# Batched matrix product on Trainium2: one store moves to GpSimd's DMA queue, and SyncE's list of transfers is regrouped into longer blocks

## Chip, cores and metric

The kernel runs on one core of a Trainium2 chip. The metric is the device time of one execution in microseconds (us). Profiles show one execution each; traces give every instruction, every DMA's issue, and the landings of its parts.

## What is computed

For each of 16 batches the kernel multiplies a 512 x 512 float32 matrix by the transpose of another. The core of the reference is

```python
batch, m, k, n = 16, 512, 512, 512
a, b: float32 (16, 512, 512)
out = np.matmul(a, b.transpose(0, 2, 1)).astype(np.float32)
```

The inputs are 33.55 MB and the output is 16.78 MB; each byte crosses between HBM and on-chip memory once. The kernel casts to bfloat16 before it multiplies and sums in float32.

## The kernel before

**Tiles.** The kernel works on 8 pairs of batches. Below, load 2u brings the two a matrices of pair u and load 2u+1 its two b matrices, so there are loads 0 to 15, each of 2 MiB. Store n writes output matrix n, 1 MiB, so there are stores 0 to 15; pair u makes outputs 2u and 2u+1. Loads 0 and 1 are issued in two halves of 1 MiB each (L98, L101), the others whole (L105). All stores are issued at L110. The landing buffer `ld` has NL = 7 slots, the output buffer `ob` has NO = 7 slots, and both are used in turn.

**Engines.** VectorE (DVE) casts each load to bfloat16 in four pieces (L155 to L163), and copies the transposed b tiles out of PSUM (L175). TensorE (PE) transposes the tiles against an identity (L235) and multiplies (L254). ScalarE (ACT) copies the transposed a tiles (L194) and the products into `ob` (L212). PE, DVE and ACT each run a loop of 8 rounds, one per pair, and meet through semaphores.

**Queues.** SyncE (SP) issues all 34 DMAs, one after another, in the order that the string ORDER spells out by hand: an L is the next load, an S the next store. Where a load reuses a slot, SP first waits on `s_cd` until DVE has begun on the load after the one that held the slot. Before store n it waits on `s_out` until n+1 outputs stand in `ob`. A waiting SP issues nothing that stands behind it in the list.

**GpSimd as messenger.** GpSimd (POOL) walks the same list. For each load it waits for the landing (`s_ld`) and passes it on to DVE as `s_go`. For each of the stores 0 to 8 it waits for the landing (`s_st`) and passes it on to ACT as `s_of`, a count of free `ob` slots. ACT starts with 7 of them and takes two ahead of each pair's output copies. GpSimd issues no DMA in the kernel before.

The lines that set the order:

```python
ORDER = "LLLLLLLSSLLLLSLSSLSLSLLSSSSSSSSS"
...
if n_ld >= NL:
    nc.sync.wait_ge(s_cd, n_ld - NL + 2)
...
nc.sync.wait_ge(s_out, n_st + 1)
nc.sync.dma_start(out[n_st]..., ob[:, slot]).then_inc(s_st[slot], 16)
```

Of the kernel before, what the change touches and what calls it, by code (L numbers as in the profile page):

```python
# [10 lines left out]
def kernel(  # L11
# [6 lines left out]
    nc = tc.nc  # L18
    P = 128
    batch, M, K = a.shape  # L20
    _, N, _ = b.shape
    J = M // P
# [6 lines left out]
    NL = 7  # L29
    NO = 7  # L30


    ORDER = "LLLLLLLSSLLLLSLSSLSLSLLSSSSSSSSS"

    def sbuf(name, shape, dtype):
        return ctx.enter_context(nc.sbuf_tensor(name, shape, dtype))

    def sem(name):
        return tc.alloc_semaphore(name)

    with tc.tile_critical(no_gpsimd_drain=True):  # L41
# [8 lines left out]
        ob = sbuf("ob", [P, NO, J, N], f32)  # L50
# [3 lines left out]
        s_set = sem("s_set")  # L54
        s_ld = [sem(f"s_ld{i}") for i in range(NL)]
        s_second = [sem(f"s_second{i}") for i in range(2)]
        s_st = [sem(f"s_st{i}") for i in range(NO)]

        s_go = sem("s_go")
        s_of = sem("s_of")  # L60
# [12 lines left out]
        s_out = sem("s_out")  # L73
# [5 lines left out]
            out=ident[:], in_=ident[:], compare_op=mybir.AluOpType.not_equal, fill=1.0,  # L79
# [4 lines left out]

        n_ld = n_st = 0
        for what in ORDER:
            if what == "L":
                u, slot = n_ld // 2, n_ld % NL  # L90
# [21 lines left out]
                ).then_inc(s_st[slot], 16)  # L112
                n_st += 1
        for n in range(batch - NO, batch - 1):
            nc.sync.wait_ge(s_st[n % NO], 16 * (n // NO + 1))


        n_ld = n_st = 0
        for what in ORDER:
            if what == "L":  # L120
                got = nc.gpsimd.wait_ge(s_ld[n_ld % NL], 16 * (n_ld // NL + 1))
                if n_ld < 2:
                    got.then_inc(s_go, 1)
                    nc.gpsimd.wait_ge(s_second[n_ld], 16).then_inc(s_go, 1)
                else:
                    got.then_inc(s_go, 2)
                n_ld += 1
            else:
                if n_st < batch - NO:
                    nc.gpsimd.wait_ge(  # L130
                        s_st[n_st % NO], 16 * (n_st // NO + 1)
                    ).then_inc(s_of, 1)
                n_st += 1

# [11 lines left out]
        with nc.Fori(0, pairs, engines=[dve]) as u:  # L146
            for x, (h, w, s_c, s_w) in enumerate(
# [4 lines left out]
                if x == 0:  # L152
# [3 lines left out]
                    out=h[:, :J, :], in_=src[:, :J, :HK]  # L156
# [4 lines left out]
                    out=h[:, J:, :], in_=src[:, J:, :HK]  # L161
                ).then_inc(s_c, 1)
                nc.vector.tensor_copy(  # L163
                    out=w[:, J:, :], in_=src[:, J:, HK:]
                ).then_inc(s_w, 1)
            for ko in range(KO):
# [5 lines left out]
                if ko == 1:  # L172
# [3 lines left out]
                    out=tb[:, ko, :],  # L176
# [9 lines left out]
        with nc.Fori(0, pairs, engines=[act]) as u:  # L186
            for ko in range(KO):
# [5 lines left out]
                for e in range(2):  # L193
                    c = nc.scalar.copy(  # L194
                        out=ta[:, ko, e * J * P:(e + 1) * J * P].rearrange(
                            "k (j p h) -> k j p h", j=J, h=2
                        ),
# [6 lines left out]
            for e in range(2):  # L204
                dst = ob[:, bass.ds((u * 2 + e) % NO, 1)].rearrange("m o j n -> m (o j) n")
                for j in range(J):
                    if j < J - 1:
                        nc.scalar.wait_ge(s_mm, j + 1)
                    else:
# [3 lines left out]
                        out=dst[:, j, :].rearrange("m (p j) -> m p j", j=2 * J),  # L213
# [51 lines left out]


    with tc.tile_critical(no_gpsimd_drain=True):
        nc.sync.wait_ge(s_st[(batch - 1) % NO], 16 * ((batch - 1) // NO + 1))


# [28 lines left out]
```

## Time and profile before

| what | value |
|---|---|
| median of 4 runs | 127.22 us (127.1 to 127.5) |
| profiled execution, its own time | 127.38 us |
| its span, first to last instruction | 125.6 us |
| time around the span in that execution | 1.78 us |
| DMA queue of SyncE | 50.33 MB, 96.1% of 16 DMA engines' span |
| mean rate over the span | 401 GB/s |
| PE / DVE / ACT / POOL busy | 74% / 56% / 54% / 1% |
| last store: issued, landed | 116.0 us, 124.2 us |

Busy shares are averages over the span. The time is read against the profiled execution's own 127.38 us: the span and the 1.78 us around it.

### The profile page before, as it was taken

The numbers are of one execution on the slowest core, as the hardware profiler recorded it, in microseconds if no ns is written. First come the engines' busy times: TensorE is split into PE (matmuls) and PEld (weight loads), VectorE is DVE, ScalarE is ACT, GpSimd is POOL, SyncE is SP. The second block draws the span as 40 slices with busy tenths as digits, with TensorE's granted clock in tenths as the row PEclk, the third lists the DMA queues.
The fourth block names the chain that finished last, engine by engine and source line by source line (L and its number), as shares of the span: only waits on it lengthen the run. The fifth ranks groups of instructions, "written<-read, shape, count | busy, mean of one in ns | idle before, by whom it ended". The sixth has DMA issues, their size and how long they took to land. (4 is left out here: it accounts for less than half of the span.)

```text
span 125.6 us, 2407 instructions
## 1 busy us (share of the span) xinstructions
PE 93.2 (74%) x768; PEld 58.6 (47%) x768; DVE 70.3 (56%) x112; ACT 68.3 (54%) x130; POOL 0.7 (1%) x6
## 2 busy tenths in 40 slices
PE   0005299998999899799989998995079998997000
PEld 0005296457447644664475467443078447642000
DVE  0056676937992891988768568370486858500000
ACT  4004133669558946965595679568106559566000
POOL 2000000000000000000000000000000000000000
PEclk9999999999999999999999999999757999999965
DMA  3999999999999999999999999999999999999970
GB/s 89 399 425 433 444 438 418 433 428 433 438 295 397 446 391 438 428 433 423 423 428 444 397 454 397 384 451 418 438 428 438 412 418 433 423 425 425 428 321 18
DMA packets 4896, 50.33 MB, mean 401 GB/s; under 512 B 544, under 2 KB 544, under 8 KB 544
## 3 DMA queue, kind: packets, MB, share of 16 engines
q1 hardware_dynamic: 4896, 50.33, 96.1%
HBM read 33.55 MB, written 16.78 MB: 401 GB/s over the span
## 5 line engine op out<-in xcount | busy, mean ns | idle before, releaser
L254 PE MATMUL ps<-tb,ta 128*128 128x512 bf16 x256 | 58.1, 381 | 0.4
L212 ACT COPY ob<-ps 128x512 f32 x64 | 34.7, 588 | 26.9 <-PE ps L254 26.9
L194 ACT COPY ta<-tp 128x512 bf16<-128x512 bf16 x64 | 32.9, 604 | 19.8 <-PE tp L235 19.8
L254 PEld LDWEIGHTS ps<-tb,ta 128*128 128x128 bf16 x256 | 24.4, 98 | 30.7 <-issue 4.1
L235 PE MATMUL tp<-ident,ha 128*128 128x128 bf16 x256 | 20.2, 236 | 12.8 <-PEq L136 12.5
L235 PE MATMUL tp<-ident,hb 128*128 128x128 bf16 x256 | 19.8, 239 | 8.8 <-PEq L136 8.7
L235 PEld LDWEIGHTS tp<-ident,ha 128*128 128x128 bf16 x256 | 17.5, 106 | 16.0 <-issue 14.4
L175 DVE COPY tb<-tp 128x1024 bf16<-128x1024 bf16 x32 | 21.3, 685 | 5.5 <-DVEq L136 5.4
L235 PEld LDWEIGHTS tp<-ident,hb 128*128 128x128 bf16 x256 | 17.6, 108 | 9.5 <-issue 9.5
L155 DVE CAST hb<-ld 128x1024 bf16 x8 | 5.5, 693 | 12.7 <-DVEq L136 12.5
L155 DVE CAST ha<-ld 128x1024 bf16 x8 | 5.5, 689 | 9.5 <-DVEq L136 9.4
L170 DVE COPY ha<-wa 128x2048 bf16<-128x2048 bf16 x8 | 5.6, 694 | 8.4 <-DVEq L136 8.1
L160 DVE CAST hb<-ld 128x1024 bf16 x8 | 5.5, 686 | 1.1 <-DVEq L136 1.1
L160 DVE CAST ha<-ld 128x1024 bf16 x8 | 5.5, 686 | 1.0 <-DVEq L136 1.0
L174 DVE COPY hb<-wb 128x2048 bf16<-128x2048 bf16 x8 | 5.5, 685 | 0.5 <-DVEq L136 0.5
L158 DVE CAST wa<-ld 128x1024 bf16 x8 | 5.5, 686 | 0.0
L163 DVE CAST wa<-ld 128x1024 bf16 x8 | 5.5, 685 | 0.0
L158 DVE CAST wb<-ld 128x1024 bf16 x8 | 5.5, 685 | 0.0
L163 DVE CAST wb<-ld 128x1024 bf16 x8 | 5.5, 685 | 0.0
L185 ACT ACT_TABLE_LOAD x1 | 1.3, 1283 | 1.1 <-SPq L41 1.1
L78 POOL TENSOR_SCALAR_AFFINE_SELECT ident<-ident 128x128 bf16<-128x128 bf16 x1 | 0.3, 294 | 0.2 <-POOL ident L76 0.2
L76 POOL MEMSET ident<- 128x128 bf16 x1 | 0.2, 205 | 0.5 <-SPq L41 0.5
(5 smaller groups left out, 0.6 us busy)
## 6 DMA issues: line engine op xcount, KB each, us to landing
out_dram<-ob SPq DMA_DIRECT2D x16, 1024.0 KB, 27.6
ld<-in_a_dram SPq DMA_DIRECT2D x7, 2048.0 KB, 30.5
ld<-in_b_dram SPq DMA_DIRECT2D x7, 2048.0 KB, 29.5
ld<-in_a_dram SPq DMA_DIRECT2D x2, 1024.0 KB, 6.4
ld<-in_b_dram SPq DMA_DIRECT2D x2, 1024.0 KB, 10.4
```

The costliest lines, as they stand in the source:

```text
L155: nc.vector.tensor_copy(out=h[:, :J, :], in_=src[:, :J, :HK]).then_inc(s_cd, 1)
L158: nc.vector.tensor_copy(out=w[:, :J, :], in_=src[:, :J, HK:])
L160: nc.vector.tensor_copy(out=h[:, J:, :], in_=src[:, J:, :HK]).then_inc(s_c, 1)
L163: nc.vector.tensor_copy(out=w[:, J:, :], in_=src[:, J:, HK:]).then_inc(s_w, 1)
L170: nc.vector.tensor_copy(out=ha[:], in_=wa[:]).then_inc(s_ca, 1)
L174: nc.vector.tensor_copy(out=hb[:], in_=wb[:]).then_inc(s_cb, 1)
L175: nc.vector.tensor_copy(out=tb[:, ko, :], in_=tp[:, 2 + ko % 2].rearrange("k j p -> k (j p)"),).then_inc(s_eb, 1)
L185: nc.scalar.copy(out=one[:], in_=nc.const_aps.tensor(1.0, (P, 1), f32))
L194: c = nc.scalar.copy(out=ta[:, ko, e * J * P:(e + 1) * J * P].rearrange("k (j p h) -> k j p h", j=J, h=2), in_=tp[:, ko % 2, :, e * HP:(e ...
L212: c = nc.scalar.copy(out=dst[:, j, :].rearrange("m (p j) -> m p j", j=2 * J), in_=ps[:, j, :].rearrange("m (j p) -> m p j", j=2 * J),)
L235: t = nc.tensor.transpose(tp[:, 2 * x + g, j, :], h[:, j, g * P:(g + 1) * P], ident[:])
L254: t = nc.tensor.matmul(ps[:, j, :], ta[:, ko, (e * J + j) * P:(e * J + j + 1) * P], tb[:, ko, :].rearrange("k (j p) -> k j p", j=2 * J)[:, ...
```

## The change

Store 0 is taken out of SP's list. GpSimd issues it: after it has passed on load 3 it waits until output 0 is in `ob` (`s_out` at 1), starts the DMA on its own queue with a semaphore of its own (`s_first`), goes on to loads 4 to 6, and after load 6 waits for the landing of store 0 and passes that on to ACT.

SP's list becomes 9 loads, stores 1 to 3, 5 loads, stores 4 to 6, 2 loads, stores 7 to 15. Since slot 0 of `ob` has one store fewer on its semaphore, a small function gives the count that marks a landing. Tiles, casts, transposes, products and copies are as before.

```diff
-    ORDER = "LLLLLLLSSLLLLSLSSLSLSLLSSSSSSSSS"
+    ORDER = "LLLLLLLLLSSSLLLLLSSSLLSSSSSSSSS"
...
+        s_first = sem("s_first")
...
+        def landed(n):
+            return 16 * (n // NO + (n % NO > 0))
...
-        n_ld = n_st = 0
+        n_ld, n_st = 0, 1
...
                     got.then_inc(s_go, 2)
                 n_ld += 1
+                if n_ld == 4:
+                    nc.gpsimd.wait_ge(s_out, 1)
+                    nc.gpsimd.dma_start(
+                        out[0].rearrange("(p j) n -> p j n", j=J), ob[:, 0]
+                    ).then_inc(s_first, 16)
+                elif n_ld == NL:
+                    nc.gpsimd.wait_ge(s_first, 16).then_inc(s_of, 1)
...
-                        s_st[n_st % NO], 16 * (n_st // NO + 1)
+                        s_st[n_st % NO], landed(n_st)
```

More of the change, by code (lines that the diff above doesn't have):

```diff
@@ L114 @@
         for n in range(batch - NO, batch - 1):
-            nc.sync.wait_ge(s_st[n % NO], 16 * (n // NO + 1))
-        n_ld = n_st = 0
+            nc.sync.wait_ge(s_st[n % NO], landed(n))
+        n_ld, n_st = 0, 1
         for what in ORDER:
@@ L267 @@
     with tc.tile_critical(no_gpsimd_drain=True):
-        nc.sync.wait_ge(s_st[(batch - 1) % NO], 16 * ((batch - 1) // NO + 1))
+        nc.sync.wait_ge(s_st[(batch - 1) % NO], landed(batch - 1))
 _INS = ['a', 'b']
```

## The prediction

> **What bounds the kernel now.** I read the page's engine shares and DMA line first, then the time in windows, then SyncE's waits and issues.
>
> ```profile
> PE 93.2 (74%) x768; PEld 58.6 (47%) x768; DVE 70.3 (56%) x112; ACT 68.3 (54%) x130; POOL 0.7 (1%) x6
> ...
> DMA  3999999999999999999999999999999999999970
> GB/s 89 399 425 433 444 438 418 433 428 433 438 295 397 446 391 438 428 433 423 423 428 444 397 454 397 384 451 418 438 428 438 412 418 433 423 425 425 428 321 18
> ...
> q1 hardware_dynamic: 4896, 50.33, 96.1%
> ```
>
> No compute engine is over 74% busy, while the 16 DMA engines are at 9 tenths or more from slice 2 to the last but one. So the kernel is one stream of 48 MiB, and its time is the stream's length. The stream works first in, first out: loads 2 to 5 land at 18.63, 23.52, 28.43 and 33.33 us, 4.90 us per 2 MiB, and in the last nine stores 2.46 us go by per MiB (means over 16 parts). A transfer takes its bytes and nothing besides. Only dips in the rate lengthen the stream. These are windows over them (columns: window, us, busy of PE, PEld, DVE, ACT, POOL, clock, DMA share, GB/s):
>
> ```profile
> 34.30:37.50 3.20, 3.20 (x17) 1.45 (x15) 3.20 (x6) 1.92 (x4) 0.00 (x0) 1.00 1.03 328
> 44.30:46.30 2.00, 1.94 (x10) 0.81 (x9) 2.00 (x5) 1.07 (x2) 0.00 (x0) 1.00 0.98 352
> 66.50:68.00 1.50, 1.50 (x16) 0.84 (x13) 1.19 (x2) 1.01 (x3) 0.00 (x0) 1.00 1.10 459
> 76.40:79.40 3.00, 2.81 (x37) 2.12 (x36) 2.50 (x5) 2.62 (x6) 0.00 (x0) 1.00 0.96 363
> 8.00:34.30 26.30, 20.61 (x171) 14.58 (x172) 18.10 (x30) 13.08 (x26) 0.00 (x0) 1.00 1.01 431
> 84.00:86.00 2.00, 2.00 (x17) 1.10 (x15) 0.79 (x2) 1.40 (x4) 0.00 (x0) 1.00 1.02 434
> 90.00:94.00 4.00, 2.28 (x22) 2.31 (x23) 3.56 (x7) 0.00 (x0) 0.00 (x0) 0.50 1.01 434
> ```
>
> The undisturbed rate is 431. In the dips the share stays near 1: engines hold load packets that take longer, they don't stand idle. The lost time is 3.20 x (1 - 328/431) = 0.76 us at 34 us, 2.00 x (1 - 352/431) = 0.37 at 44 us, 3.00 x (1 - 363/431) = 0.47 at 76 us, 1.6 in sum. The first lies within load 6, before any store moves. The other two lie 1 to 3 us behind a block of two stores (0 and 1; 3 and 4). Behind single stores (2, 5 and 6: windows at 66, 84 and 90) nothing is lost.
>
> ```profile
> SPq L110 <- ACT ob L212: 89.0, 16, 20.4
> SPq L105 <- DVE ha L155: 3.4, 1, 3.4
> ...
> 26.21 2.52 SPq L110 DMA_DIRECT2D out_dram<-ob  x2
> ...
> 63.53 52.84 SPq L110 DMA_DIRECT2D out_dram<-ob  x9
> ```
>
> SP waits 89 us for outputs, and it costs nothing: what it issues then waits in the stream anyway (27.6 us from issue to landing in the median store). The last two stores are issued at 113.86 and 116.04 us and land 7.9 and 8.2 us later. An empty queue needs 5.35 us (first half load, 0.94 to 6.29). So output 15 could come 8.2 - 5.35 = 2.8 us later without moving the end.
>
> **What the Trainium skill says.** The page "DMA: Bandwidth & Descriptors", section "Issuing engines are not separate DMA queues", says that transfers from SP, ACT and GpSimd run on the same 16 engines and interleave. The trace before has one queue alone, so the sharing isn't shown; that the engines are full is (96.1%). Its section "Queues, rings and completion order" says that an engine takes turns between queues, packet by packet; no run here shows it yet. The page "SBUF — State Buffer", section "SBUF: two separate sides", says that a GpSimd DMA's descriptors wait while VectorE holds the shared port in a two-port copy. In the trace DVE's casts end at 26.36 us and its next work starts at 28.68, so store 0's issue near 26.2 meets a free port. The page "TensorE: Matmul & The Clock Gate", Part 1, says that the clock halves after an idle window of about 3.4 us. The trace agrees: after PE idles 5.08 us up to 91.72, the 90 to 94 window has clock 0.50.
>
> **The change, part by part.** The sum is made against the profiled execution: 125.6 + 1.78 around it = 127.38 us, 0.16 over the median. I apply the difference to the median, 127.22.
>
> *Bytes and issues.* 48 MiB stay 48 MiB. SP loses one issue of 0.34 us and one wait, POOL gains them; both stand beside the full stream. Cost 0.
>
> *Cover of SP's new order.* Loads 7 and 8 leave earlier: their slots are free at about 12.3 and 21.9 us (DVE's casts of loads 1 and 2), against 28.78 and 29.25. Then SP waits for stores 1, 2, 3 (28.4, 37.7, 39.9 us) and all of loads 9 to 13 stand behind that. By 39.9 the stream has moved about 15 of the 22 MiB issued, so 7 x 2.45 = 17 us of work cover the wait. The next block, stores 4 to 6, is issued by about 61 us with some 12 MiB ahead of it. Load 15 waits for the cast of load 9, near 65 us; the stream then has 10 MiB left. No gap, cost 0. Were this cover gone, each us of SP's wait would be a us of time.
>
> *Store 0 on GpSimd.* POOL waits from load 3 (23.5 us) until output 0 at 26.2; load 4 lands at 28.43 and its casts start at 32.87, so 4 us hide it. Its 1 MiB goes in turns with load packets from about 27 to 35 us; load 5 slips from 33.3 to about 35.8. Pair 2's transposes of b start at 39.82, the four casts take 2.8, so this is hidden too. Bounds for its own cost to the stream: upper 0.4 us, an estimate from the first-byte times in the same DMA page's "Latency and other measured facts" (about 1 us against 0.6), if engines stood idle for it, which loads behind them speak against; lower -0.76, if its packets filled the first dip, although they should be through before most of it. I take 0.
>
> *Later landings for ACT.* Load 9 moves from MiB 22 to 24 of the stream (59.2 to 64 us), store 4 from 29 to 33 (76.5 to about 86.5). ACT's copies of pair 5 began at 80.32; they now wait for slot 4, until about 86.7. Eight copies with PE between them took 6.2 us there; with the first products ready some 5.2 suffice, so pair 5 ends near 92 instead of 86.53. Load 13 is 2 MiB earlier (34 to 32, near 84 us), so pair 6 starts at once and, at a pair per 11.51 us (transposes start at 38.93 and 50.44), ends near 103.5, against 104.51. Pair 7 hangs on load 15, MiB 39 in both orders, so it ends near 116 again. If PE idles into a half-clock window on the way (3.4 us more), about 118.4, within the 2.8 us. Cost 0.
>
> *Switches of direction.* 11 changes between loads and stores become 5 in SP's list. By themselves they cost nothing visible: DMA share and rate hold through 82 to 90 us, where four of them lie. What cost time were dips behind blocks: pairs 0.37 + 0.47 = 0.84, singles 0. Now there are two blocks of three ahead of loads. Lower bound: a block of three costs what one of two does, 0.42 each, 0.84 in all, difference 0. Upper: the third store adds as much again as the second, 0.84 each, 1.68, difference +0.84. I take the middle, +0.42, as no row decides. The dip of 0.76 in load 6 has no store ahead of it, and I let it stand.
>
> Sum: 0 + 0 + 0 + 0 + 0.42, so 127.22 + 0.42 = 127.6 us.
>
> **Rivals.** *Nothing moves.* Dips saturate with two stores, or are HBM's own and come with load bytes, which are the same: 127.2 us. For it: the dip in load 6 needs no store. Against: all others follow pairs.
>
> *Faster, by fewer and shorter dips* (the other side). The dip before the first store block, 0.76 us, is tied to how the first stores meet the loads, or store 0's packets fill it: 127.22 - 0.76 = 126.5. Or the cost is per return to loads: 0.84 over five returns is 0.17, two remain, -0.5, 126.7. For it: the dip ends just as the first stores begin. It decides from the point that dips in the after add up to less than 1.4 us. Against: singles cost nothing, so a cost per switch does not fit.
>
> *Compute catches up with the stream.* The wait for store 4 and two half-clock windows (2 x 3.4 us) take pair 7's end from 116 to 122.8; less the 2.8 of slack, +4 us at most; half of that is 129.2. It decides once output 15 is later than 118.8 us. Against: load 13's earlier landing gives most of it back.
>
> That the change doesn't do what it says is hardly possible: the order of issues is written out.
>
> **How the numbers follow.** Longer dips (127.3 to 128.4, likeliest 127.6): 0.42. Nothing: 0.20. Faster: 0.33. Compute: 0.05. About 0.2%, 0.25 us, is what a measurement of this kernel can tell from no change. Faster 0.33, same 0.20, slower 0.42 + 0.05 = 0.47. The range takes in the faster case to 126.3 (126.5 less the 0.2 by which runs vary) and the longer dips with their upper bound, 0.84, and the 0.4 of GpSimd's first byte: 127.22 + 1.24 = 128.5. The likeliest case's own range is 127.3 to 128.4.
>
> **What would show it.** Right: DMA share full throughout; the rate under 380 for some 3 us after stores 1 to 3 (around 60 us) and after 4 to 6 (around 92); last issue near 116. Wrong: a queue beside q1 whose packets take much longer than 0.31 us per 8 KB; no dips after the blocks; 34 to 38 us at 430 GB/s; a gap in the DMA line near 40 or 60 us; the last store issued after 118.8.

## The result, and the profile after

The changed kernel takes 127.05 us (median of 42 runs, 126.24 to 127.57) against 127.47 us for the kernel before on the same chips (63 runs, 126.53 to 128.44; the 127.22 on record was the median of the first four). The ratio is 0.9969, with a 95% interval of 0.9955 to 0.9984: faster by 0.31%, some 0.4 us; small, but the interval leaves out 1. The forecast was slower, 127.6.

The profiled execution took 126.81 us, its span is 125.0. These are the shares and the DMA line of its page:

```profile
PE 92.4 (74%) x768; PEld 57.6 (46%) x768; DVE 70.1 (56%) x112; ACT 68.2 (55%) x130; POOL 1.4 (1%) x7
...
DMA  3999999999999999999999999999999999999970
GB/s 84 396 425 448 430 430 430 435 430 364 417 425 435 451 425 401 425 425 427 409 440 440 419 430 425 425 414 422 438 414 430 406 419 433 425 427 425 422 309 31
...
q1 hardware_dynamic: 4752, 49.29, 94.0%
q0 software_dynamic: 144, 1.05, 2.0%
```

The kernel is the same full stream as before. GpSimd's queue is q0: 2.0% of the span is 2.5 us per engine for 1 MiB, what a store on SP's queue takes too. The slice of 295 GB/s (slice 12 before) is gone; a shallower one, 364, stands in slice 10, from 28 us on, around the start of store 0, whose own packets run beside the loads from 29.79 to 37.72 us. The windows over the dips (columns as before: window, us, PE, PEld, DVE, ACT, POOL busy, clock, DMA share, GB/s):

```profile
8.00:28.00 20.00, 14.92 (x117) 10.78 (x118) 12.93 (x20) 8.64 (x17) 0.67 (x1) 1.00 1.01 432
28.00:33.50 5.50, 4.95 (x57) 3.36 (x55) 4.89 (x8) 4.21 (x9) 0.00 (x0) 1.00 1.00 387
34.30:37.50 3.20, 3.20 (x16) 1.44 (x15) 2.21 (x4) 2.05 (x4) 0.00 (x0) 1.00 1.00 428
57.80:60.80 3.00, 3.00 (x16) 1.35 (x15) 0.02 (x1) 2.15 (x4) 0.00 (x0) 1.00 0.98 377
90.60:92.60 2.00, 2.00 (x34) 1.82 (x32) 0.47 (x1) 1.87 (x4) 0.00 (x0) 1.00 1.03 401
```

Against 431 GB/s, as in the prediction, the losses are 0.56 us (28 to 33.5), 0.02 (34 to 37.5), 0.38 behind stores 1 to 3 and 0.14 behind stores 4 to 6: 1.1 us, where the kernel before lost 1.6. The dip in load 6 has not stayed, and the dips behind the blocks of three did not grow.

SyncE's issues after (start, us, queue, line, count; merged rows include the waits between):

```profile
12.26 0.33 SPq L110 DMA_DIRECT2D ld<-in_b_dram  x1
21.70 0.33 SPq L110 DMA_DIRECT2D ld<-in_a_dram  x1
27.83 11.84 SPq L115 DMA_DIRECT2D out_dram<-ob  x3
...
64.85 0.34 SPq L110 DMA_DIRECT2D ld<-in_b_dram  x1
```

Loads 7, 8 and 15 leave at 12.26, 21.70 and 64.85 us, and no slice of the DMA line falls below 9 in between: SP's long waits are covered.

### The profile page after: what moved, and what is told of

The parts are those of the page before. It is cut to its first block, busy times and chain, and to the rows that moved or that the text cites. A ratio compares the mean times of both kernels' runs of the same rounds, so it can differ in the third digit from the quotient of the medians.

```text
span 125.0 us, 2407 instructions
## 1 busy us (share of the span) xinstructions
PE 92.4 (74%) x768; PEld 57.6 (46%) x768; DVE 70.1 (56%) x112; ACT 68.2 (55%) x130; POOL 1.4 (1%) x7
## 5 line engine op out<-in xcount | busy, mean ns | idle before, releaser
L247 PE MATMUL tp<-ident,hb 128*128 128x128 bf16 x256 | 19.1, 234 | 7.6 <-PEq L148 7.5
L247 PEld LDWEIGHTS tp<-ident,hb 128*128 128x128 bf16 x256 | 17.1, 106 | 8.3 <-issue 8.3
L135 POOL DMA_DIRECT2D out_dram<-ob x1 | 0.7, 668 | 24.2 <-ACT ob L224 24.2
## 6 DMA issues: line engine op xcount, KB each, us to landing
out_dram<-ob SPq DMA_DIRECT2D x15, 1024.0 KB, 21.9
```

The lines of the kernel that those rows point to most:

```text
L247: t = nc.tensor.transpose(tp[:, 2 * x + g, j, :], h[:, j, g * P:(g + 1) * P], ident[:])
```

## The experiments

Three questions were put: which half of the change gives the gain, whether dips follow the order or chance, and what the first one hangs on. "Dip" below is the time lost in a window, its length times (1 - rate/431), from one profile of each kernel. Ratios are against the kernel before on the same chip, with 95% intervals.

The windows are picked by eye and leave things out. From 37.5 to 41 us, where stores 0 and 1 run in the kernel before, its two profiles show 389 and 410 GB/s, which is another 0.34 and 0.17 us that the table does not count. So a measure that picks nothing stands beside them: the landing of store 15, the last. It has 16 parts. Their mean says how long the stream took, and the execution ends some time after the last part. The column gives the mean, and how far behind it the last part came.

| kernel | what differs from before | first dip | all dips | store 15 lands: mean + last part behind it | ratio | interval |
|---|---|---|---|---|---|---|
| before, two profiles | | 0.76, 0.82 | 1.60, 1.26 | 122.28 + 1.94, 122.08 + 1.60 | 1 | |
| changed kernel, two profiles | both halves | 0.56, 0.45 | 1.08, 0.89 | 121.72 + 1.93, 121.64 + 1.94 | 0.9969 | 0.9955 to 0.9984 |
| blocks_only | SP's list alone | 0.26 | 0.85 | 121.81 + 1.77 | 0.9966 | 0.9948 to 0.9985 |
| pool_only | store 0 on GpSimd alone | 0.56 | 1.13 | 121.73 + 2.26 | 0.9952 | 0.9919 to 0.9984 |
| act_loads | second queue without GpSimd | 0.33 + 0.28 | 1.16 | 121.76 + 1.50 | 0.9953 | 0.9929 to 0.9978 |
| alternate | seven single stores, 7 returns | 0.73 | 1.38 | 122.04 + 1.93 | 0.9987 | 0.9972 to 1.0002 |
| eight_first | first store behind 8 loads | 1.01 | 2.15 | 122.49 + 1.35 | 0.9981 | 0.9960 to 1.0001 |
| nine_first | first store behind 9 loads | 0.38 | 1.32 | 121.93 + 1.93 | 0.9979 | 0.9961 to 0.9998 |
| prewrite | 64 KB stored early | 0.65 | 1.38 | 122.34 + 2.63 | 1.0003 | 0.9977 to 1.0029 |
| pool_early | stores 0 to 6 on GpSimd | 0.45 | 0.50 | 121.52 + 1.17 | 0.9895 | 0.9874 to 0.9916 |
| pool_spread | the same, stores 4 to 6 later | 0.38 | 0.53 | 121.16 + 1.89 | 0.9892 | 0.9868 to 0.9916 |

(The 0.28 of act_loads lies from 37.5 to 41 us, the stretch that is not counted for the others.) In the changed kernel's two profiles the mean comes 0.36 to 0.64 us earlier than in the two of the kernel before. The trace's packets say where: those of loads 2 to 15 took 70.1 and 70.0 us per engine in the kernel before and 69.6 in both profiles of the changed one, those of the stores 39.7 in all four.

### Each half alone

```diff
# blocks_only, in the kernel before
-    ORDER = "LLLLLLLSSLLLLSLSSLSLSLLSSSSSSSSS"
+    ORDER = "LLLLLLLLLSSSSLLLLLSSSLLSSSSSSSSS"
# pool_only, in the changed kernel
-    ORDER = "LLLLLLLLLSSSLLLLLSSSLLSSSSSSSSS"
+    ORDER = "LLLLLLLSLLLLSLSSLSLSLLSSSSSSSSS"
```

> The regrouped list alone: store 0 goes back into SyncE's list, at the head of its first block, so 9 loads, 4 stores, 5 loads, 3 stores, 2 loads, 9 stores, no DMA on GpSimd. Against 127.47 us for the kernel before. If the gain comes from fewer returns from stores to loads (2 in place of 5): 127.0, and a dip before the first store remains. If it comes from store 0 going beside the loads: no gain, 127.4 to 127.5. If longer blocks cost more, as the prediction had it (a block of four 1.0 to 1.3 us of dip behind it): 127.9 or more.

> Store 0 alone on GpSimd's queue, the rest of SyncE's list as in the kernel before less its first store: 7 loads, store 1, 4 loads, store 2, load, stores 3 and 4, and so on. If the gain comes from store 0 beside the loads: 127.0, and load 6 shows no dip. If it comes from fewer returns to loads: no gain, 127.4 to 127.5, since the 5 returns stay.

Measured: 127.04 and 126.65 us against 127.38. Each half alone gives about the whole gain, and the two do not add up: the intervals of all three kernels overlap. Their windows between 28 and 47 us, first blocks_only, then pool_only:

```profile
34.30:37.50 3.20, 3.20 (x16) 1.46 (x15) 3.17 (x6) 1.92 (x5) 0.00 (x0) 1.00 1.00 425
44.30:46.80 2.50, 2.48 (x12) 1.19 (x13) 2.50 (x5) 1.33 (x3) 0.00 (x0) 1.00 1.05 387
```

```profile
28.00:33.50 5.50, 4.95 (x55) 3.28 (x53) 4.97 (x9) 4.21 (x10) 0.00 (x0) 1.00 0.99 387
34.30:37.50 3.20, 3.20 (x17) 1.45 (x15) 2.18 (x4) 2.13 (x4) 0.00 (x0) 1.00 1.01 430
```

Both lack the dip at 34 us. In blocks_only it has moved with the first store to load 8, and is smaller (0.26 us); in pool_only it lies around the start of store 0 beside the loads (0.56). What is left later, 0.59 and 0.57 us, differs little, though blocks_only returns twice to loads and pool_only five times. Blocks of four and three stores (0.38 and 0.21 behind them) cost no more than pairs did: the prediction's "longer blocks" is refuted here.

### Order or chance, returns or pairs

before_again and after_again are the two kernels unchanged, for a second profile.

> The kernel before, unchanged, for a second profile of it. If dips sit where the order of transfers puts them: again a dip of 0.7 to 0.9 us in load 6, near 34 to 37 us, ahead of the first store, and some 0.3 us each behind stores 1 and 4. If dips come by chance: in other loads, of other sizes.

> The changed kernel, unchanged, for a second profile of it. If dips sit where the order puts them: again about 0.5 us of longer load packets between 28 and 33 us, where store 0 goes beside the loads, none at 34 to 37, about 0.3 behind store 3 near 58 us and 0.2 behind store 6 near 91. If by chance: elsewhere.

The line of the first dip in before_again:

```profile
34.30:37.50 3.20, 3.20 (x17) 1.42 (x16) 2.87 (x5) 2.08 (x4) 0.00 (x0) 1.00 1.00 320
```

The dips came again in the same places: before 0.82, 0.37 and 0.07 us, after 0.45, 0.30 and 0.14. The large ones hold their size; the one at 76 us does not (0.47, then 0.07). The profiled execution of before_again took 126.84 us, about as long as those of the changed kernel (126.81 and 126.75): its mean landing is later than theirs, but its last part came only 1.60 us behind the mean. A single execution's time therefore does not tell the kernels apart; the medians and the mean landings do.

The next kernel, stream_before, has no computation at all; DVE only fills the output buffer once, which shifts the stream by 15 us, and it takes 142.29 us.

```diff
-                    nc.sync.wait_ge(s_cd, n_ld - NL + 2)
+                    nc.sync.wait_ge(s_ld[slot], 16 * (n_ld // NL))
...
-                nc.sync.wait_ge(s_out, n_st + 1)
```

> Leaves out all the computation: no casts, transposes, products or copies, the stores send a constant, and loads wait only for the landing of the load that held their slot. SyncE's list is that of the kernel before. If dips come from the order of loads and stores in the stream: dips of the same size in load 6 and behind the store pairs, 1.5 us in sum. If they come from the engines' work beside the stream, or from what waits on it: no dips but at the start.

Its windows (window, us, DVE, POOL busy, clock, DMA share, GB/s):

```profile
23.00:49.00 26.00, 0.00 (x0) 0.00 (x0) 1.00 1.02 433
49.00:53.00 4.00, 0.00 (x0) 0.00 (x0) 1.00 0.95 303
59.00:62.00 3.00, 0.00 (x0) 0.00 (x0) 1.00 1.01 366
64.00:80.00 16.00, 0.00 (x0) 0.00 (x0) 1.00 1.01 433
```

15 us later than in the kernel before come a first dip (49 to 53 for 34 to 38) and one behind the pair (59 to 62 for 44 to 47), with PE, DVE and ACT idle. They are 1.19 and 0.45 us, not smaller than the 0.76 and 0.37 of before. So the dips belong to the order of loads and stores in the stream, not to the engines' work beside it.

alternate spreads the first seven stores singly:

```diff
-    ORDER = "LLLLLLLSSLLLLSLSSLSLSLLSSSSSSSSS"
+    ORDER = "LLLLLLLSLSLSLSLSLSLLSLLSSSSSSSSS"
```

> The kernel before with its first seven stores each alone between loads, 7 returns to loads and no pair of stores ahead of a load, nothing on GpSimd. If each return costs some 0.15 us: slower than before by about 0.3 us, 127.8. If only blocks of two and more cost, as the prediction had it: the 0.84 us behind the pairs go, 126.7. If dips come by chance whatever the order: 127.4 to 127.5 with dips anywhere in the loads.

127.13 us against 127.38, not told from no change. Its dips are 0.73 ahead of the first store, then 0.26, 0.25 and 0.14 behind stores 0, 1 and 2, and none behind stores 3 to 6 (427 GB/s from 70 to 78 us). The window behind store 0:

```profile
41.00:44.00 3.00, 2.81 (x34) 1.81 (x30) 2.50 (x5) 2.32 (x5) 0.00 (x0) 1.00 1.02 393
```

Single stores do cost, if they are early. Neither the number of returns alone nor the length of a block alone sets the price. Being late does not make a return free either: the pair of stores 3 and 4, near 76 us, costs 0.30 to 0.47 us in six of the seven profiles that have it there, and 0.07 in before_again (skewed and skew_clean, which come below, apart). No rule that holds in all profiles was found.

### What the first dip hangs on

eight_first and nine_first move only the place of the first pair of stores:

```diff
-    ORDER = "LLLLLLLSSLLLLSLSSLSLSLLSSSSSSSSS"
+    ORDER = "LLLLLLLLSSLLLSLSSLSLSLLSSSSSSSSS"    # eight_first
+    ORDER = "LLLLLLLLLSSLLSLSSLSLSLLSSSSSSSSS"    # nine_first
```

> The kernel before with one load moved: 8 loads ahead of the first two stores and 3 behind them, all else the same, 5 returns, nothing on GpSimd. If the gain hangs on where the first store meets the loads (a dip that the first store of the list causes, smaller when that store comes later): faster by 0.3 to 0.4 us, about 127.1. If it hangs on the number of returns or on block lengths: no gain, 127.4 to 127.5.

> The kernel before with two loads moved: 9 loads ahead of the first two stores and 2 behind them, all else the same, 5 returns, nothing on GpSimd. The regrouped list alone had its first dip in load 8 and only half as large (0.39 us against 0.85). If the place of the first store decides: a dip of about 0.4 us in load 8, and 127.1 us. If the block length behind it decides (four stores there, two here): a dip of 0.8 in load 8, as with 8 loads first in load 7 (0.81), and 127.4.

The dips of 0.39, 0.85 and 0.81 us in the second expectation are counted by packets: the time that load packets in the dip took over their usual 0.611 us, per engine. These are the windows of the first dips, eight_first's and then nine_first's:

```profile
39.00:43.00 4.00, 3.45 (x43) 2.34 (x41) 3.50 (x7) 3.25 (x7) 0.00 (x0) 1.00 0.95 322
44.30:47.00 2.70, 2.70 (x14) 1.27 (x13) 2.70 (x6) 1.87 (x4) 0.00 (x0) 1.00 1.01 370
```

127.23 us against 127.56, not told from no change, and 127.06 against 127.38, just told from it. The first dip follows the store each time, to 39 to 43 us and to 44 to 47. It is 1.01 us behind eight loads, not smaller than behind seven, and 0.38 behind nine. So nine loads ahead of the store halve the dip with no long block behind it. But the dips behind the stores are then larger (0.94 in sum, against 0.59 in blocks_only); the gain, 0.21%, is not told from that of blocks_only, 0.34%.

eight_first has more dips than the kernel before and yet is no slower. Its landings resolve this for its one profile: the mean is the latest of the kernels without added transfers, 122.49 us, as its dips would have it, but the last part came only 1.35 us behind it, where before had 1.94 and 1.60. In that execution the parts were already closer together at load 2, ahead of every store: 0.31 us against 0.63 and 0.50.

prewrite stores 64 KB of zeros to a corner of output 15, behind load 3; the whole of output 15 is stored over it later.

```diff
+                if n_ld == 4:
+                    nc.sync.wait_ge(s_fill, 1)
+                    nc.sync.dma_start(
+                        out[batch - 1].rearrange("(p j) n -> p j n", j=J)[:, 0, :P], pre[:]
+                    ).then_inc(s_pre, 16)
```

> The kernel before with a small extra store: 64 KB of zeros to a corner of output 15 go out right behind load 3, near 23 us, and output 15 is stored over it at the end. The 64 KB themselves add about 0.2 us to the stream. If the dip in load 6 is a cost of the very first write to HBM, paid once: it moves to 20 to 24 us, and load 6 at 34 to 37 us runs at the full 430 GB/s. If it belongs to the first full store behind a row of loads: it stays at 34 to 37 us and the time is 0.2 above that of before, 127.6.

127.66 against 127.56 us. 426 GB/s from 20 to 25 us, and 343 from 34.3 to 37.5: the dip stays. It isn't the price of the first write to HBM as such, at least not of a small one.

act_loads gives the first loads to ScalarE's queue, so that SP's first stores need not stand behind them:

```diff
+                queue = nc.scalar if n_ld < NL else nc.sync
...
-                    nc.sync.dma_start(ld[:, slot], src).then_inc(s_ld[slot], 16)
+                    queue.dma_start(ld[:, slot], src).then_inc(s_ld[slot], 16)
```

> The kernel before with loads 0 to 6 issued by ScalarE ahead of its other work, all else by SyncE in the order of before, nothing on GpSimd. Stores 0 and 1 then go beside loads 4 to 6 on a second queue that is not GpSimd's. If a second queue is what makes the first store cheap: longer load packets of 0.4 to 0.5 us around 27 to 33 us, none at 34 to 37, and 126.7 to 127.1. If it takes GpSimd's queue: a dip of 0.8 us and no gain, 127.4.

126.7 us against 127.5, and no dip at 34 to 37.5 us:

```profile
34.30:37.50 3.20, 3.20 (x16) 1.47 (x15) 2.01 (x4) 2.05 (x4) 0.00 (x0) 1.00 1.01 430
```

So a second queue gives the gain without GpSimd issuing anything.

skewed and skew_clean put three small loads on 8 of the 128 partitions behind load 4, to set some engines back:

```diff
+                if n_ld == 5:
+                    for i in range(4, NO):
+                        nc.sync.dma_start(
+                            ob[:8, i], a[0, :8 * J].rearrange("(p j) k -> p j k", j=J)
+                        ).then_inc(s_skew, 16)
```

They land in slots 4 to 6 of `ob`, which ACT may use only afterwards. skew_clean reads rows 520 apart instead (about 1 MiB).

> The kernel before with three small extra loads behind load 4: 8 KB on each of 8 partitions, to output slots not yet in use, so that some of the 16 engines fall behind the others by up to 0.93 us; added work, nothing left out. If dips arise because the engines go in step (spread of a landing under 1 us) when they change from loads to stores and back: the first dip, 0.8 us in load 6, shrinks to under 0.3, and the time is at most 127.5 in spite of 0.5 us of added packets. If the order alone makes the dip: it stays at 0.8 us and the time goes to 128 or more.

> As skewed, but the small extra loads (8 KB on each of 8 partitions, three times) read rows of the input that lie about 1 MiB apart, so that they should not hinder each other; added work, nothing left out. If the first dip is paid once, when engines first come apart: the small loads take it, little or nothing of it is left in load 6 before the first store at 38 us, and the sum of longer load packets is 1.2 us or less. If the first full store causes it: 0.8 us in load 6 as in the kernel before, on top of what the small loads cost.

130.18 and 130.46 us, ratios 1.023 (1.0194 to 1.0266) and 1.0209 (1.0178 to 1.024). As a saving, the idea failed: the small loads stretch the packets around them, whichever of the two sets of rows they read. Windows of skew_clean:

```profile
26.50:31.50 5.00, 4.51 (x62) 3.44 (x59) 3.79 (x7) 4.40 (x9) 0.00 (x0) 1.00 1.01 203
34.30:37.50 3.20, 3.20 (x17) 1.43 (x16) 0.47 (x1) 1.91 (x5) 0.00 (x0) 1.00 1.01 430
45.50:48.00 2.50, 2.50 (x13) 1.15 (x12) 0.73 (x2) 1.22 (x4) 0.00 (x0) 1.00 1.07 406
```

The price is 2.65 us at 26.5 to 31.5, but afterwards load 6 runs at 430 with the first stores right behind it, and the dip behind the pair is down to 0.15 us. Both kernels show this. That fits a price paid once, by whatever disturbs the stream first. It does not show that the price is for the engines coming apart, which was the idea. How far a load's last part lands behind the mean of its 16 parts tells how far apart they are. Across the first dip this grew in the kernel before (0.64 to 0.99 us, in the second profile 0.50 to 0.66), but it shrank in eight_first (0.31 to 0.24), nine_first (0.31 to 0.21) and blocks_only (0.32 to 0.24), and jumped there only one step later, at the first load behind the stores, to 0.80, 0.69 and 0.92. What the first dip pays for stays open.

### A faster version

pool_early issues stores 0 to 6 from GpSimd as they become ready, SP has 16 loads and then 9 stores; pool_spread holds stores 4 to 6 back until load 11 has landed. GpSimd's list of what it waits for and issues (L: pass on a load, i: issue a store, w: pass on its landing):

```diff
+        for what in (
+            "L L L L i0 L i1 L i2 i3 w0 w1 L L i4 i5 w2 w3 L L i6 L w4 w5 L w6 L L L L w7 w8"
+        ).split():
...
+            if what[0] == "i":
+                nc.gpsimd.wait_ge(s_out, n + 1)
+                nc.gpsimd.dma_start(
+                    out[n].rearrange("(p j) n -> p j n", j=J), ob[:, n]
+                ).then_inc(s_early[n], 16)
```

> Stores 0 to 6 all on GpSimd's queue as soon as they are ready, SyncE issues 16 loads and then stores 7 to 15: no return from a store to a load in SyncE's list. If a store beside loads costs less than a store between them: faster than after, 126.6 or less. If the gain of the change came from the list's longer blocks: about the changed kernel's time, 127.0. If sharing an engine between two queues costs something for each store (0.5 us of dip lay in the 28 to 34 us of the changed kernel): 0.5 for each of seven, about 130.

> Stores 0 to 3 on GpSimd's queue as they become ready, stores 4 to 6 there too but only from the landing of load 11 on, so that loads 5 to 13 are held up less; SyncE issues 16 loads and stores 7 to 15. If stores beside loads spare the dips behind returns, and the kernel with seven early stores on GpSimd was held at its end by late outputs (last store issued at 117.4 us): last store issued by 116.5 and 125.8 us or less. If late outputs were not its limit: 126.2, as there.

126.16 us (0.9895, 0.9874 to 0.9916) and 126.09 us (0.9892, 0.9868 to 0.9916): 1.3 us faster than the kernel before, 0.9 than the changed one. The windows of pool_early:

```profile
27.00:33.50 6.50, 5.95 (x61) 3.78 (x58) 5.96 (x10) 4.80 (x10) 0.53 (x1) 1.00 1.00 401
38.80:41.00 2.20, 1.71 (x28) 1.42 (x26) 2.20 (x4) 2.20 (x5) 0.57 (x1) 1.00 1.03 421
45.00:60.00 15.00, 11.96 (x102) 7.04 (x101) 8.90 (x15) 8.98 (x18) 1.19 (x2) 1.00 1.00 427
60.00:80.00 20.00, 16.48 (x127) 10.46 (x125) 11.52 (x19) 11.23 (x22) 0.58 (x1) 0.91 1.01 431
82.00:98.00 16.00, 15.45 (x146) 11.04 (x146) 11.91 (x20) 10.07 (x20) 0.00 (x0) 0.89 1.02 438
```

The first store beside the loads costs 0.45 us, the six others little (0.05 us at 38.8 to 41, 0.14 at 45 to 60), and there are no returns. In pool_early the last store lands 5.33 us after its issue at 117.36, as on an empty queue, so its end waits for outputs. pool_spread issues it at 116.91, and its mean landing is 0.36 us earlier, but the last part comes 1.89 us behind instead of 1.17, and the medians are the same. So with the earlier last output the stream was shorter and the execution was not. Whether the wider spread comes from the order or from chance, one profile each can't tell.

## Why the prediction was wrong

It was wrong in sign: +0.4 us forecast, -0.4 measured. Two steps failed, both on dips.

- *"the third store adds as much again as the second ... I take the middle, +0.42"*: refuted. Behind the blocks of three the changed kernel lost 0.38 and 0.14 us (0.30 and 0.14 in its second profile), 0.52 in place of the 1.26 that the step implies. The kernel before lost 0.84 there, and 0.44 in its second profile, so the term is between -0.3 and 0, not +0.42. "Singles 0" came from three single stores of one profile: alternate's early ones cost 0.26 and 0.25 us, and store 2 alone, which cost nothing in before, costs 0.32 in eight_first and 0.22 in nine_first near 66 us. The step took the length of a block for the cause, where the block's place counts as well.
- *"The dip of 0.76 in load 6 has no store ahead of it, and I let it stand"*: refuted. It had a store behind it. It moves with the first store (eight_first, nine_first), and it shrank to 0.56 and 0.45 us when store 0 went beside the loads: -0.2 to -0.4 for a term put at 0.

Together the dips fell from 1.60 and 1.26 us to 1.08 and 0.89 in two profiles each, by 0.45 us in the mean, for a measured 0.4 us. The mean landing of store 15 agrees without any choice of windows: 0.50 us earlier. So the gain is a shorter stream. Counted by load packets over 0.611 us, some 0.36 of it lie in the first dip and 0.15 in all the rest.

The rival *faster, by fewer and shorter dips* came true with its first mechanism, "how the first stores meet the loads", at about half its 0.76 us. Its threshold held (1.1 us, under 1.4). Store 0's packets did not fill the dip, as it also offered: they brought a smaller one of their own. Its other mechanism, a price per return, did not hold: five returns cost 0.57 us in pool_only, two cost 0.59 in blocks_only.

What held:

- *Cover of SP's order*, cost 0: SP issued loads 7, 8 and 15 at 12.26, 21.70 and 64.85 us for the 12.3, 21.9 and 65 forecast; the stream never ran dry.
- *Store 0 on GpSimd*, own cost 0: q0's packets take 2.5 us per engine. Load 5 landed at 35.45 (35.8 forecast). What it did to the other packets is the first dip, which the step's lower bound of -0.76 allowed for and its value left out. The Trainium skill's page "DMA: Bandwidth & Descriptors" says in "Queues, rings and completion order" that an engine takes turns between queues, packet by packet. The trace after agrees: from 29.79 to 37.72 us, 140 packets of loads start among the 128 of store 0. The free port was misjudged: DVE's last cast ended at 26.32, and GpSimd's issue began at 25.92. The issue took 0.67 us nevertheless, and no run shows what a longer overlap would cost.
- *Later landings for ACT*, cost 0. These are ACT's rows around pair 5 in the changed kernel (start, us, line, count, idle before):

```profile
86.21 2.05 ACT L224 COPY ob<-ps 128x512 f32 x4 [3.29 <-PE ps L266]
89.06 1.07 ACT L224 COPY ob<-ps 128x512 f32 x2 [0.80 <-PE ps L266]
90.73 1.09 ACT L224 COPY ob<-ps 128x512 f32 x2 [0.60 <-PE ps L266]
```

The copies begin at 86.21 us, just behind the landing of store 4 at 85.90 (86.7 forecast). The row names PE, but pair 5's first products had been ready for some 2 us; the wait is for the slot. Pair 5 ends at 91.82 (92), pair 6 at 103.33 (103.5), pair 7 at 115.47 (116), and the last store is issued at 115.49, so the compute rival found no room.

One reading of the prediction's is off without effect: its landing times for loads 2 to 5 are those of the last of 16 parts; the means are 18.00, 22.89, 27.79 and 32.68, again 4.90 us apart.

What stays open: why load packets take longer ahead of a first store and behind stores, why nine loads ahead of the first store halve the first dip when eight don't, and whether the two halves of the change differ at all; their intervals overlap.

## What to carry to other kernels

In a kernel held by its DMA stream, look for windows where the engines' share stays full and the rate falls: here such time was lost in load packets that took longer, and it moved with the order of loads and stores. Before pricing a reordering from such dips, ask of each where it lies and what comes right behind it as well as ahead of it; two or three dips don't tell length from position, and a second profile can show which of them hold. Check the sum of hand-picked windows against a measure of the whole stream, such as the mean landing of the last store, and look apart from it at how far the last part comes behind. Here, stores issued from a second queue beside the loads left one small dip and avoided those behind stores.

## What the runs showed of the hardware

- Load packets slow down up to 3 us ahead of the first store's own packets: 328 and 320 GB/s at 34.3 to 37.5 us in the kernel before, where the first store packet starts at 37.54 and 37.43; with no computation 303. In the first of these profiles 36 of the 64 load packets in that window took over 0.70 us, up to 1.57, against 0.61 elsewhere.
- Three small loads on 8 partitions cut the stream to 203 and 210 GB/s for 5 us: 2.65 and 2.56 us lost for 192 KB.
- With stores from GpSimd beside SP's loads the stream of pool_early kept 427 and 431 GB/s from 45 to 80 us: after the first of them, they cost it little.
- The 16 parts of one transfer drift apart: in the kernel before, the last part lands 0.63 us behind their mean at load 2 and 1.94 us at store 15. The execution waits for the last.
